# RWKV-7 and dilated attention layer on one core: the RWKV heads' small products alternate between halves of TensorE's array, updates are read out once per two chunks, and low-rank low parts have the full height

## The chip, the cores and the metric

One core of a Trainium2 chip. The core has TensorE (PE, matrix products; PEld is its loading of weights), VectorE (DVE), ScalarE (ACT), GpSimd (POOL), and SyncE (SP), which issues most DMAs. The metric is the time of one execution on the device in microseconds (us), the median of several runs.

## The reference

A decoder layer for 2048 tokens of 1024 channels: eight RWKV-7 heads and eight heads of dilated attention side by side, an output projection, and a SwiGLU feed-forward. The change touches the RWKV heads alone; their core is a recurrence over tokens:

```python
def step(state, inp):
    r_t, w_t, k_t, v_t, kk_t, a_t = inp
    sa = jnp.einsum('bhij,bhj->bhi', state, -kk_t)
    state = (state * w_t[:, :, None, :]
             + sa[..., :, None] * (kk_t * a_t)[..., None, :]
             + v_t[..., :, None] * k_t[..., None, :])
    y = jnp.einsum('bhij,bhj->bhi', state, r_t)
    return state, y
...
w = -jax.nn.softplus(-(w0 + jnp.tanh(xw) @ w2)) - 0.5
decay = jnp.exp(-jnp.exp(w.astype(jnp.float32)))
a = jax.nn.sigmoid(a0 + xa @ a2)
```

`w2` and `a2` are low-rank products: 64 channels in, 512 out.

## The kernel before

The tokens are taken in 4 blocks of 512. TensorE's order is written out by hand: `drive` lays two streams into one. The dense stream (`dense_in`: input projection, in float32r products of 128 x 128 by 512 columns; three products, `three`, for each pair of high and low parts) fills the time in which the messy stream (`rwkv`) waits for other engines. A step of the messy stream yields the dense time to put before the next one (Y_T, CH_X and so on, in us); these numbers set the order, whatever the products really take. The other engines' instructions are ordered by a scheduler. When the dense stream ends, during the last block's chunks, attention becomes the other stream.

The heads go through TensorE as 4 pairs; a pair holds one head in channels 0 to 63 and one in 64 to 127 (e = 0, 1). For each block and pair:

- `start_pair` makes decay and learning rate (lines 519 to 526): a product at full height with the high part of `w2`, one on half the height (64 rows) with its low part `wa_lo`, and the same for `a2`.
- The T blocks (L638): products over 64 rows, 128 columns wide, for each of 8 chunks of 64 tokens, in 4 batches (e = 0, 1; chunks 0 to 3, 4 to 7) of 4 products. Each batch writes one tile `tp` of the pool `ps_t`, which has two buffers and serves other small products too. Two ScalarE copies (L645, L646) and two VectorE products with triangle masks (L648, L652) empty it.
- After an inversion on VectorE, merges (L705, L718) of 32 x 32 blocks: 4 batches a block, each 16 products on rows 0 to 31 and then 16 on rows 64 to 95.

Then the chain over the 8 chunks. A chunk has five groups of products, 8 each (4 pairs, e = 0, 1): `xp` (L804, all rows, column half e), the readout of the state `ye[e]` (L819, row half e, column half by the chunk's parity q), `up_` (L829, row half e, column half e), the new state `s_ps` (L842, all rows, column half e), and the readout of the updates, into the same `ye[e]` (L861, all rows, column half q). VectorE turns `s_ps` into the state for the next chunk (L848, L857, tile `suv`), for which the next `xp` waits. A product of float32 operands is two instructions on TensorE.

Of the kernel before, what the change touches and what calls it, by code (L numbers as in the profile page):

```python
# [9 lines left out]
F32 = mybir.dt.float32  # L10
# [8 lines left out]
P = 128  # L19
# [22 lines left out]
def f32(ap):  # L42
    return ap.bitcast(F32)
# [3 lines left out]
def tile_hybrid_layer(  # L47
# [29 lines left out]
    # TensorE takes its instructions as they come here: the two streams are laid out below.  # L77
# [22 lines left out]
    # Additive masks over [previous block | own block], and over the own block in the order of  # L100
    # the second branch with the keys of the third: same residue mod 4, not later.
    amask = cst.tile([P, 2 * P], BF16, name="amask")
    mask4 = cst.tile([P, P // 4, 4], BF16, name="mask4")

    def build_masks():
        res = cst.tile([P, 4], F32, name="res")
        nc.vector.tensor_reduce(out=res, in_=ident.rearrange("p (a c) -> p c a", c=4), axis=AX.X, op=ALU.max)
        nc.vector.tensor_scalar(out=res, in0=res, scalar1=-1.0, scalar2=-NEG, op0=ALU.add, op1=ALU.mult)
        nc.vector.tensor_copy(out=mask4, in_=res.unsqueeze(1).to_broadcast([P, P // 4, 4]))
        nc.gpsimd.memset(amask, 0.0)  # L110
        m4 = mask4.rearrange("p a c -> p (a c)")
        for m, sign in ((amask[:, 0:P], 1), (amask[:, P:], -1), (m4, -1)):
            nc.gpsimd.affine_select(
                out=m, in_=m, pattern=[[sign, P]], base=0, channel_multiplier=-sign,
                compare_op=ALU.is_ge, fill=NEG,
            )

    # Per-channel vectors, one row per 128 channels, turned to columns.
# [20 lines left out]
    def rms_inv(pool, ss, scale, eps, who):  # L139
        """(ss * scale + eps) ** -0.5 on [128, n]."""  # L140
# [38 lines left out]
    class Weights:  # L179
        """Pieces of weights in the order of their use: loaded and split ahead of it."""  # L180
# [57 lines left out]
    # Constants of this part.  # L238
# [7 lines left out]
    ones64 = chp.tile([P, CH], F32, name="ones64")  # L246
    maskS = chp.tile([P, CH], F32, name="maskS")
    maskI = chp.tile([P, CH], F32, name="maskI")
    headsel = sp.tile([P, 2], F32, name="headsel")
    reset = sp.tile([P, TB], BF16, name="reset")  # L250
# [3 lines left out]
    wa_lo = sp.tile([P, W], F32R, name="wa_lo")  # L254
# [10 lines left out]
    def constants():  # L265
# [5 lines left out]
        # high parts twice, low parts of one beside those of the other  # L271
        for hi, src, tag, lo in ((w2d, decay_w2[0], "L", slice(0, HD)), (a2d, iclr_a2[0], "kkh", slice(HD, P))):
# [4 lines left out]
            nc.vector.tensor_tensor(out=wa_lo[lo], in0=raw[lo], in1=f32(hi[lo]), op=ALU.subtract)  # L277
# [7 lines left out]
        nc.gpsimd.memset(reset, 1.0)  # L285
        nc.gpsimd.memset(reset.rearrange("p (c t) -> p c t", t=CH)[:, :, 0:1], 0.0)
# [3 lines left out]
        nc.gpsimd.memset(ones64, 1.0)  # L290
        for m, base in ((maskS, -1), (maskI, 0)):
            for h in range(2):
                # keep t - s + base >= 0
# [63 lines left out]
    def dense_in():  # L357
# [58 lines left out]
        for b in range(nblocks):  # L416
            t0 = b * TB
            for at, ct in enumerate(ORDER):
# [26 lines left out]
                if b == 0 and at == 6:  # L445
                    build_masks()
# [1226 lines left out]
```

## Time and profile before

| what | value |
|---|---|
| median of 3 timed runs | 3056.62 us |
| the runs | 3053.95 to 3061.08 us |
| profiled execution, its span | 3063.5 us |
| TensorE busy | 2966.2 us, 97% of the span |
| VectorE, ScalarE, GpSimd busy | 1959.1, 1407.3, 383.5 us |
| granted TensorE clock, mean | 0.981 |

The span is the profiled execution's own time from its first to its last instruction; no time around it is known, and it is 6.9 us longer than the median of the runs without profile. Busy time of TensorE is an upper bound: products are pipelined, and their ends are modelled.

### The profile page before, as it was taken

The numbers are of one execution on the slowest core, as the hardware profiler recorded it, in microseconds if no ns is written. First come the engines' busy times: TensorE is split into PE (matmuls) and PEld (weight loads), VectorE is DVE, ScalarE is ACT, GpSimd is POOL, SyncE is SP. The second block draws the span as 40 slices with busy tenths as digits, with TensorE's granted clock in tenths as the row PEclk, the third lists the DMA queues.
The fourth block names the chain that finished last, engine by engine and source line by source line (L and its number), as shares of the span: only waits on it lengthen the run. The fifth ranks groups of instructions, "written<-read, shape, count | busy, mean of one in ns | idle before, by whom it ended". The sixth has DMA issues, their size and how long they took to land.

```text
span 3063.5 us, 47429 instructions
## 1 busy us (share of the span) xinstructions
PE 2966.2 (97%) x17457; PEld 2449.3 (80%) x17457; DVE 1959.1 (64%) x3974; ACT 1407.3 (46%) x2688; POOL 383.5 (13%) x540
## 2 busy tenths in 40 slices
PE   8999999999998888899999999999999999999998
PEld 6777787787787776788888888888888888888887
DVE  6778777776776886675765676566575544454444
ACT  5434534444444665675554455444454323342223
POOL 1113113203102321100110111001011100000001
PEclk9999999999998898899999999999999999999999
DMA  4332332231232578554544345443434333343333
GB/s 124 90 98 76 90 97 73 85 105 58 68 94 81 158 226 251 174 139 117 145 125 144 114 126 162 122 127 97 135 118 145 98 108 98 100 121 97 97 97 103
DMA packets 456716, 358.67 MB, mean 117 GB/s; under 512 B 26610, under 2 KB 384548, under 8 KB 456484
## 3 DMA queue, kind: packets, MB, share of 16 engines
q1 hardware_dynamic: 419348, 318.35, 35.2%
q10 hardware_dynamic: 32656, 22.62, 2.4%
q0 software_dynamic: 4480, 14.68, 1.3%
q8 instruction: 137, 2.24, 0.3%
q14 instruction: 95, 0.78, 0.1%
HBM read 311.19 MB, written 44.37 MB: 116 GB/s over the span
## 4 chain that ended last, share of the span: by engine, by line
PE 56%; DMA 3%; DVE 2%; ACT 1%; issue 1%; POOL 0%; SPq 0%; ACTq 0%; DVEq 0%; POOLq 0%
PE acc L214 6%; PE acc L216 6%; PE acc L215 6%; PE pg L214 5%; PE pu L214 5%; PE pg L216 5%; PE pu L216 5%; PE pu L215 5%; PE pg L215 5%; PE po L963 3%; PE pt_att L949 2%; PE s_att L932 1%; PE s_att L933 1%; DMA rq<-qT 1%; DMA rk_all<-kT 1%
## 5 line engine op out<-in xcount | busy, mean ns | idle before, releaser
L202 DVE TENSOR_TENSOR wlo<-wraw,whi 128x512 fp32r<-128x512 f32 x800 | 564.6, 707 | 631.1 <-ACT whi L200 623.5
L200 ACT CAST whi<-wraw 128x512 fp32r<-128x512 f32 x800 | 495.0, 619 | 961.1 <-PE acc L216 251.1
L214 PE MATMUL pd<-h_hi,whi 128*128 128x512 f32 (+1 forms) x840 | 357.0, 425 | 2.9 <-DVE r L456 1.5
L216 PE MATMUL pd<-h_hi,wlo 128*128 128x512 f32 (+1 forms) x840 | 332.0, 395 | 0.0
L215 PE MATMUL pd<-h_lo,whi 128*128 128x512 f32 (+1 forms) x840 | 331.0, 394 | 0.9 <-DVE h_lo L374 0.6
L214 PE MATMUL acc<-whi,a_hi 128*128 128x512 f32 x704 | 286.6, 407 | 0.6 <-DVE x L1487 0.5
L214 PE MATMUL pg<-fh_hi,whi 128*128 128x512 f32 x704 | 284.1, 404 | 1.0 <-DVE x L1487 0.6
L214 PE MATMUL pu<-fh_hi,whi 128*128 128x512 f32 x704 | 284.6, 404 | 0.0
L216 PE MATMUL pg<-fh_hi,wlo 128*128 128x512 f32 x704 | 275.9, 392 | 0.2 <-DVE wlo L202 0.2
L216 PE MATMUL acc<-whi,a_lo 128*128 128x512 f32 x704 | 276.0, 392 | 0.0
L216 PE MATMUL pu<-fh_hi,wlo 128*128 128x512 f32 x704 | 275.8, 392 | 0.0
L215 PE MATMUL pg<-fh_lo,whi 128*128 128x512 f32 x704 | 274.6, 390 | 0.0
L215 PE MATMUL acc<-wlo,a_hi 128*128 128x512 f32 x704 | 274.5, 390 | 0.0
L215 PE MATMUL pu<-fh_lo,whi 128*128 128x512 f32 x704 | 274.4, 390 | 0.0
L942 ACT ACTIVATE pr<-pr,mx 128x256 f32<-128x256 f32 (+1 forms) x416 | 162.5, 449 | 102.6 <-DVE mx L937 102.4
L214 PEld LDWEIGHTS pd<-h_hi,whi 128*128 128x128 f32 x840 | 160.3, 191 | 43.7 <-issue 3.6
L216 PEld LDWEIGHTS pd<-h_hi,wlo 128*128 128x128 f32 x840 | 160.0, 191 | 35.4
L215 PEld LDWEIGHTS pd<-h_lo,whi 128*128 128x128 f32 x840 | 160.7, 191 | 27.1 <-DVE h_lo L374 2.2
L969 POOL COPY oo<-mx 128x2 f32<-128x2 f32 (+2 forms) x160 | 51.6, 328 | 996.2 <-DVE mx L937 888.6
L963 PEld LDWEIGHTS po<-vv,pts 128*128 128x128 f32 x1008 | 152.6, 196 | 21.7 <-ACT oo L968 2.6
L216 PEld LDWEIGHTS pg<-fh_hi,wlo 128*128 128x128 f32 x704 | 132.1, 188 | 30.0 <-DVE wlo L202 1.0
L216 PEld LDWEIGHTS pu<-fh_hi,wlo 128*128 128x128 f32 x704 | 132.1, 188 | 29.4 <-DVE wlo L202 0.3
(578 smaller groups left out, 5684.0 us busy)
## 6 DMA issues: line engine op xcount, KB each, us to landing
wraw<-in_w_in_dram SPq DMA_DIRECT2D x208, 256.0 KB, 2.9
wraw<-in_w_gate_dram SPq DMA_DIRECT2D x176, 256.0 KB, 2.9
wraw<-in_w_up_dram SPq DMA_DIRECT2D x176, 256.0 KB, 2.9
wraw<-in_w_down_dram SPq DMA_DIRECT2D x176, 256.0 KB, 2.6
rq<-qT SPq DMA_DIRECT2D x128, 128.0 KB, 3.6
wraw<-in_w_out_dram SPq DMA_DIRECT2D x64, 256.0 KB, 3.1
rk_all<-kT SPq DMA_DIRECT2D x48, 256.0 KB, 4.2
rk_all<-kT SPq DMA_DIRECT2D x80, 128.0 KB, 3.4
```

Source lines behind the costliest of these rows:

```text
L200: nc.scalar.copy(out=hi, in_=raw)
L202: nc.vector.tensor_tensor(out=lo, in0=raw, in1=f32(hi), op=ALU.subtract)
L214: nc.tensor.matmul(ps, lhsT=lhs[0], rhs=rhs[0], start=first, stop=False)
L215: nc.tensor.matmul(ps, lhsT=lhs[0], rhs=rhs[1], start=False, stop=False)
L216: nc.tensor.matmul(ps, lhsT=lhs[1], rhs=rhs[0], start=False, stop=last)
L932: nc.tensor.matmul(ps[:, g, :], lhsT=q, rhs=kh, start=True, stop=False)
L933: nc.tensor.matmul(ps[:, g, :], lhsT=q, rhs=kl, start=False, stop=True)
L942: nc.scalar.activation(out=pr[:, g, :], in_=pr[:, g, :], func=AF.Exp, scale=-1.0, bias=mx[:, g])
L949: nc.tensor.transpose(pt[:, g, kb, :], pr[:, g, kb * P : (kb + 1) * P], ident)
L963: nc.tensor.matmul(po[:, g, :], lhsT=pts[:, g, kb, :], rhs=vb[g][kb], start=(kb == 0), stop=(kb == kbs - 1))
L969: nc.gpsimd.tensor_copy(out=o[:, :, OA:OW], in_=self.mxs[j])
```

## The change

The core of the difference; lines that only lose comments, or get new numbers, are left out.

```diff
-                nc.tensor.matmul(zp, lhsT=wa_lo[0:HD, js], rhs=xwa[0:HD, 0], start=False, stop=True)
+                nc.tensor.matmul(zp, lhsT=w2lo[:, js], rhs=xwa[:, 0], start=False, stop=True)
...
-                nc.tensor.matmul(ap_, lhsT=wa_lo[HD:P, js], rhs=xwa[HD:P, 1], start=False, stop=True)
+                nc.tensor.matmul(ap_, lhsT=a2lo[:, js], rhs=xwa[:, 1], start=False, stop=True)
...
-                for e in range(2):
-                    es = slice(e * HD, (e + 1) * HD)
-                    ks = slice((1 - e) * HD, (2 - e) * HD)
-                    for c0 in range(0, NCH, 4):
-                        tp = ps_t.tile([P, 4, 2, CH], F32, name="tp", tag="t")
-                        for c in range(4):
+                for c0 in range(0, NCH, 4):
+                    tps = [ps_t.tile([P, 4, 2, CH], F32, name="tp", tag="t") for _ in range(2)]
+                    for c in range(4):
+                        for e, tp in enumerate(tps):
+                            es = slice(e * HD, (e + 1) * HD)
                             nc.tensor.matmul(
                                 tp[:, c, :, :], lhsT=BK[es, c0 + c, :, :],
                                 rhs=Wj[es, c0 + c, 2 * e : 5 : 4 - 2 * e, :], start=True, stop=True,
                             )
...
-                        yield Y_T
+                    yield Y_T2
...
-                for e in range(2):
-                    r0 = e * HD
-                    for u in range(U2):
+                for u in range(U2):
+                    for r0 in (0, HD):
                         nc.tensor.matmul(
                             qp[r0 + 32 : r0 + 64, u, :], lhsT=TAB[r0 : r0 + 32, g + u, 32:64],
...
-                    for j in range(NPAIR):
+                for j in range(NPAIR):
+                    for e in range(2):
+                        es = slice(e * HD, (e + 1) * HD)
                         nc.tensor.matmul(
                             ye[e][qs, j, :], lhsT=Wt[j][es, c, 4, :], rhs=now[es, j, e, :],
...
-                for e in range(2):
-                    for j in range(NPAIR):
-                        nc.tensor.matmul(
-                            ye[e][qs, j, :], lhsT=Wt[j][:, c, 2 * e + 1, :], rhs=now[:, j, e, :],
-                            start=False, stop=True, skip_group_check=True,
-                        )
+                if q == 1:
+
+                    for e in range(2):
+                        for j in range(NPAIR):
+                            for cc, of in ((c - 1, before), (c, now)):
+                                nc.tensor.matmul(
+                                    ye[e][(cc % 2) * CH : (cc % 2 + 1) * CH, j, :],
+                                    lhsT=Wt[j][:, cc, 2 * e + 1, :], rhs=of[:, j, e, :],
+                                    start=False, stop=True, skip_group_check=True,
+                                )
+                before = now
```

Y_T2 is 1.6, twice Y_T. The low parts `w2lo` and `a2lo` have 128 rows, of which GpSimd sets the other 64 to zero at the start. The second merge (`mp`) alternates like the first. The triangle masks become bf16 and the reset of the decay's running sum becomes bytes. Attention's masks, built in the first block before, are built in attention's own pool where attention begins.

TensorE's order at the first pair's T blocks (L638, in the change L647; `tp` is their tile, `pd` the dense stream's). Before:

```order
L638 MATMUL tp<-W_547,BK 128x128 x4
L214 MATMUL pd<-h_hi,whi 128x512
L215 MATMUL pd<-h_lo,whi 128x512
L216 MATMUL pd<-h_hi,wlo 128x512
...
L638 MATMUL tp<-W_547,BK 128x128 x4
...
L666 MATMUL tp_788<-ident,BK 128x128 x4
```

In the change:

```order
L647 MATMUL tp<-W_548,BK 128x128 x8
L221 MATMUL pd<-h_hi,whi 128x512
L222 MATMUL pd<-h_lo,whi 128x512
L223 MATMUL pd<-h_hi,wlo 128x512
...
L647 MATMUL tp<-W_548,BK 128x128 x8
...
L677 MATMUL tp_775<-ident,BK 128x128 x4
```

Before, 6, 3 and 3 dense products stood between the four batches and 3 before the transposes; now 9 stand between the two batches and 6 before the transposes.

VectorE's order in the same place (L648 and L652, in the change L659 and L663, empty `tp`; L202, now L209, splits weights; `kx` and `mshift` belong to the dense stream). Before:

```order
L648 TENSOR_TENSOR W_547<-tp,maskS 64x4x64
L652 TENSOR_TENSOR W_547<-tp,maskI 128x4x64
L580 SCALAR_TENSOR_TENSOR tmp<-r,vec,tmp 128x512
L648 TENSOR_TENSOR W_547<-tp,maskS 64x4x64
L652 TENSOR_TENSOR W_547<-tp,maskI 128x4x64
L202 TENSOR_TENSOR wlo<-wraw,whi 128x512
L456 SCALAR_TENSOR_TENSOR kx<-pd,omu,mshift 128x512
```

In the change:

```order
L659 TENSOR_TENSOR W_548<-tp,maskS 64x4x64
L663 TENSOR_TENSOR W_548<-tp,maskI 128x4x64
L659 TENSOR_TENSOR W_548<-tp,maskS 64x4x64
L663 TENSOR_TENSOR W_548<-tp,maskI 128x4x64
L209 TENSOR_TENSOR wlo<-wraw,whi 128x512
L466 SCALAR_TENSOR_TENSOR kx<-pd,omu,mshift 128x512
```

Both tiles of a batch are now emptied one behind the other, and the split and the dense stream's evacuation stand ahead of the next batch's masks.

TensorE's order in an even and the next odd chunk (`y_2043` and `y_2044`, in the change `y_2030` and `y_2031`, are `ye[0]` and `ye[1]`). Before, at the end of either chunk:

```order
L842 MATMUL s_ps<-suv,BKT_1396 64x64 x2
L861 MATMUL y_2043<-suv,W_547 64x64
L861 MATMUL y_2043<-suv,W_778 64x64
L861 MATMUL y_2043<-suv,W_992 64x64
L861 MATMUL y_2043<-suv,W_1213 64x64
L861 MATMUL y_2044<-suv,W_547 64x64
L861 MATMUL y_2044<-suv,W_778 64x64
```

In the change, the end of the even chunk, the next chunk's readout of the state, and the end of the odd chunk:

```order
L853 MATMUL s_ps<-suv,BKT_1383 64x64 x2
L221 MATMUL pd<-h_hi,whi 128x512
...
L830 MATMUL y_2030<-suv,W_548 64x64
L830 MATMUL y_2031<-suv,W_548 64x64
...
L853 MATMUL s_ps<-suv,BKT_1383 64x64 x2
L875 MATMUL y_2030<-suv,W_548 64x64 x2
L875 MATMUL y_2030<-suv,W_765 64x64 x2
...
L875 MATMUL y_2031<-suv,W_548 64x64 x2
```

In the even chunk dense products follow `s_ps` directly; the odd one reads out both chunks' updates.

## Rows read from the trace of the kernel before

**Rows 1.** The profile's page: its span, and engines' busy time (us, share, instructions).

```profile
span 3063.5 us, 47429 instructions
PE 2966.2 (97%) x17457; PEld 2449.3 (80%) x17457; DVE 1959.1 (64%) x3974; ACT 1407.3 (46%) x2688; POOL 383.5 (13%) x540
```

**Rows 2.** Windows: stretch, its length; busy of PE, PEld, DVE, ACT, POOL; clock, DMA.

```profile
60.00:145.00 85.00, 85.00 (x446) 66.36 (x445) 62.41 (x122) 43.94 (x93) 12.11 (x16) 1.00 0.28 84
945.00:1030.00 85.00, 71.67 (x826) 62.32 (x824) 61.01 (x160) 47.92 (x115) 27.32 (x38) 0.86 0.33 96
```

**Rows 3.** Timeline of TensorE at a T block: start, length (us), instructions merged.

```profile
64.32 0.39 PE L215 MATMUL pd<-h_lo,whi 128*128 128x512 f32 x1
64.55 0.40 PE L216 MATMUL pd<-h_hi,wlo 128*128 128x512 f32 x1
64.88 1.16 PE L638 MATMUL tp<-W,BK 64*128 64x128 f32 x8
65.96 0.50 PE L214 MATMUL pd<-h_hi,whi 128*128 128x512 f32 x1
...
67.54 1.16 PE L638 MATMUL tp<-W,BK 64*128 64x128 f32 x8
```

**Rows 4.** Timeline of the engines that empty this tile, in brackets idle time before.

```profile
65.21 0.69 DVE L202 TENSOR_TENSOR wlo<-wraw,whi 128x512 fp32r<-128x512 f32 x1
...
66.07 0.36 ACT L645 COPY TAB<-tp 32x256 f32<-32x256 f32 x1 [1.34 <-PE tp L638]
...
66.44 0.26 ACT L646 COPY TAB<-tp 32x128 f32<-32x128 f32 x1
...
66.73 0.43 DVE L648 TENSOR_TENSOR W<-tp,maskS 64x256 f32<-64x256 f32 x1 [0.83 <-ACT TAB L646]
...
67.17 0.42 DVE L652 TENSOR_TENSOR W<-tp,maskI 128x256 f32<-128x256 f32 x1
```

**Rows 5.** Timeline of TensorE, low-rank products of a pair: first, and dense product after.

```profile
41.67 0.39 PE L520 MATMUL zp<-xwa,w2d 128*128 128x512 f32 x1
...
43.28 0.51 PE L214 MATMUL pd<-h_hi,whi 128*128 128x512 f32 x1
```

**Rows 6.** Timeline of TensorE over the first chunk of the first block.

```profile
199.01 0.96 PE L819 MATMUL y<-suv,W 64*64 64x64 f32 x16
199.91 0.50 PE L214 MATMUL pd<-h_hi,whi 128*128 128x512 f32 x1
...
201.50 0.68 PE L829 MATMUL up__2073<-xs,TAB 64*64 64x64 f32 x16
202.11 0.50 PE L214 MATMUL pd<-h_hi,whi 128*128 128x512 f32 x1
...
204.38 0.69 PE L842 MATMUL s_ps<-suv,BKT 128*64 128x64 f32 x16
204.89 1.10 PE L861 MATMUL y<-suv,W 128*64 128x64 f32 x16
205.92 0.50 PE L214 MATMUL pd<-h_hi,whi 128*128 128x512 f32 x1
```

**Rows 7.** Windows within one batch of L819: length, busy (instructions in flight), clock, DMA.

```profile
208.12:208.42 0.30, 0.30 (x6) 1.00 0.00 0
208.42:208.72 0.30, 0.30 (x12) 1.00 0.00 0
```

**Rows 8.** Timeline: L857 and L804 at the first, L804 at the last of 12 chunks.

```profile
205.57 0.87 DVE L857 TENSOR_TENSOR suv<-st,s0p 64x256 f32<-64x256 f32 x2
...
207.50 0.69 PE L804 MATMUL xp<-suv,W 128*64 128x64 f32 x16
...
760.64 1.04 PE L804 MATMUL xp<-suv,W 128*64 128x64 f32 x16 [1.07 <-DVE suv L857]
```

**Rows 9.** Timeline of TensorE at the first merge batch.

```profile
181.40 2.11 PE L705 MATMUL qp<-M,TAB 32*32 32x32 f32 x64
183.44 0.50 PE L214 MATMUL pd<-h_hi,whi 128*128 128x512 f32 x1
```

More of the change, by code (lines that the diff above doesn't have):

```diff
@@ L98, in tile_hybrid_layer, with build_mask @@
     nc.gpsimd.memset(neg_half, -0.5)
[L102 to L109, printed above, removed]
+    def build_mask(pool):
+        amask = pool.tile([P, 2 * P], BF16, name="amask")
         nc.gpsimd.memset(amask, 0.0)
-        m4 = mask4.rearrange("p a c -> p (a c)")
-        for m, sign in ((amask[:, 0:P], 1), (amask[:, P:], -1), (m4, -1)):
+        for m, sign in ((amask[:, 0:P], 1), (amask[:, P:], -1)):
             nc.gpsimd.affine_select(
@@ L116, in build_masks, with build_mask4 @@
             )
+        return amask
+    def build_mask4(pool):
+        mask4 = pool.tile([P, P // 4, 4], BF16, name="mask4")
+        res = pool.tile([P, 4], F32, name="res")
+        nc.vector.tensor_reduce(out=res, in_=ident.rearrange("p (a c) -> p c a", c=4), axis=AX.X, op=ALU.max)
+        nc.vector.tensor_scalar(out=res, in0=res, scalar1=-1.0, scalar2=-NEG, op0=ALU.add, op1=ALU.mult)
+        nc.vector.tensor_copy(out=mask4, in_=res.unsqueeze(1).to_broadcast([P, P // 4, 4]))
+        m4 = mask4.rearrange("p a c -> p (a c)")
+        nc.gpsimd.affine_select(
+            out=m4, in_=m4, pattern=[[-1, P]], base=0, channel_multiplier=1, compare_op=ALU.is_ge, fill=NEG,
+        )
+        return m4
     rows = (
@@ L244, in load_gain @@
             nc.sync.dma_start(out=t, in_=mix_norm_g[0:1, h * W : (h + 1) * W].to_broadcast([P, W]))
-    ones64 = chp.tile([P, CH], F32, name="ones64")
-    maskS = chp.tile([P, CH], F32, name="maskS")
-    maskI = chp.tile([P, CH], F32, name="maskI")
+    maskS = chp.tile([P, CH], BF16, name="maskS")
+    maskI = chp.tile([P, CH], BF16, name="maskI")
     headsel = sp.tile([P, 2], F32, name="headsel")
-    reset = sp.tile([P, TB], BF16, name="reset")
+    reset = sp.tile([P, TB], mybir.dt.uint8, name="reset")
     g2 = [chp.tile([P, W], F32R, name=f"g2{part}") for part in ("hi", "lo")]
@@ L253, in tile_hybrid_layer @@
     a2d = sp.tile([P, W], F32R, name="a2d")
-    wa_lo = sp.tile([P, W], F32R, name="wa_lo")
+    w2lo = sp.tile([P, W], F32R, name="w2lo")
+    a2lo = sp.tile([P, W], F32R, name="a2lo")
     lnw = chp.tile([P, W], F32, name="lnw")
@@ L270, in constants @@
             at += n
-        for hi, src, tag, lo in ((w2d, decay_w2[0], "L", slice(0, HD)), (a2d, iclr_a2[0], "kkh", slice(HD, P))):
+        for hi, low, src, tag, lo, zero in (
+            (w2d, w2lo, decay_w2[0], "L", slice(0, HD), slice(HD, P)),
+            (a2d, a2lo, iclr_a2[0], "kkh", slice(HD, P), slice(0, HD)),
+        ):
+            nc.gpsimd.memset(f32(low[zero]), 0.0)
             raw = sp.tile([P, W], F32, name="wa_raw", tag=tag)
@@ L276, in constants @@
             nc.scalar.copy(out=hi, in_=raw)
-            nc.vector.tensor_tensor(out=wa_lo[lo], in0=raw[lo], in1=f32(hi[lo]), op=ALU.subtract)
+            nc.vector.tensor_tensor(out=low[lo], in0=raw[lo], in1=f32(hi[lo]), op=ALU.subtract)
         raw = sp.tile([P, W], F32, name="g2_raw", tag="qkv", bufs=1)
@@ L284, in constants @@
         nc.gpsimd.memset(carry, 0.0)
-        nc.gpsimd.memset(reset, 1.0)
-        nc.gpsimd.memset(reset.rearrange("p (c t) -> p c t", t=CH)[:, :, 0:1], 0.0)
+        nc.gpsimd.memset(reset, 1)
+        nc.gpsimd.memset(reset.rearrange("p (c t) -> p c t", t=CH)[:, :, 0:1], 0)
         nc.gpsimd.memset(headsel, 0.0)
@@ L289, in constants @@
         nc.gpsimd.memset(headsel[HD:P, 1:2], 1.0)
-        nc.gpsimd.memset(ones64, 1.0)
+        for m in (maskS, maskI):
+            nc.gpsimd.memset(m, 1.0)
         for m, base in ((maskS, -1), (maskI, 0)):
@@ L641, in rwkv @@
                             )
-                        us = slice(j * NCH + c0, j * NCH + c0 + 4)
+                    us = slice(j * NCH + c0, j * NCH + c0 + 4)
+                    cs = slice(c0, c0 + 4)
+                    for e, tp in enumerate(tps):
+                        ks = slice((1 - e) * HD, (2 - e) * HD)
                         h0, h1 = slice(e * HD, e * HD + 32), slice(e * HD + 32, e * HD + 64)
@@ L714, in rwkv @@
                 mp = ps_c.tile([P, U2, 32], F32, name="mp", tag="c")
-                for e in range(2):
-                    r0 = e * HD
-                    for u in range(U2):
+                for u in range(U2):
+                    for r0 in (0, HD):
                         nc.tensor.matmul(
```

13 lines of the change are left out of this document (6 added, 7 removed).

## The prediction, made before the result was known

> **What bounds the kernel now.** The page comes first: TensorE is busy for 97% of a span of 3063.5 us [rows 1]. That share says little about a single stage, so the windows by stage come next. In 60 to 145 us, where the products of the RWKV heads stand between those of the input projection, TensorE is never idle, VectorE is busy for 62.41 of 85 us and ScalarE for 43.94: no other engine is near its limit, and time taken from TensorE there comes off the span. In 945 to 1030 us, where the last head chunks run beside the first attention units, TensorE is busy for 71.67 of 85 us: it waits there, and shorter products bring little [rows 2]. So I price the edits in TensorE's own timeline, by the start of a batch and the start of what follows, since the ends are modelled and overlap.
>
> **Reading the small products.** The timeline of one T block gives the unit: dense products start 0.23 us apart, a change to products on half of the array's height costs 0.10 more (64.55 to 64.88), and a batch of 8 instructions (4 products, two instructions each) takes 1.08 us until the dense stream is back [rows 3]. In the chain stand batches of 16 small instructions. Those that alternate between halves are short: L829, whose rows and columns alternate, takes 0.61 us, and L842, whose columns alternate, 0.51. Those that stay on one half are long: L861 takes 1.03, L819 takes 0.90 [rows 6]. Without the 0.10 for the change of shape, 0.032 us an instruction against 0.058. No batch alternates rows alone, as the T blocks and L819 will, but L819 shows it once: it goes from the upper to the lower row half in its middle, and there 12 instructions are in flight in 0.3 us, against 6 at its start [rows 7]. The lower half starts while the upper still works, in the same columns. I take it that alternating row halves run at once.
>
> **T blocks.** Before, each of 16 pairs of heads (4 blocks, 4 pairs) has 4 batches: 4 x (0.10 + 1.08) = 4.72 us. After, 2 batches of 16, with 8 instructions on each half; if the halves run at once each takes what 8 took and one short step: 2 x (0.10 + 1.09) = 2.38. That frees 2.34 x 16 = 37.4 us. If they take turns, a batch of 16 costs about 2 x 1.08 - 0.20 and only the changes of shape are saved, 0.30 a batch, 9.6 us.
>
> The Trainium skill, page "TensorE: Matmul & The Clock Gate", section "Measured speedup vs the span model", gives 3.07 times for four row tiles, not four; scaled to two, 1.53 in place of 2, a batch would take some 1.37 us, an estimate. No run here shows it; the rule stands among the rivals.
>
> **What the T blocks give back.** A batch now fills both buffers of the pool at once. A tile is emptied by two ScalarE copies and then two VectorE products: the batch ends at 66.04 and the last reader at 67.59, 1.55 us later, 0.85 of it VectorE's [rows 4]. With two tiles ready together, the second waits for VectorE: 1.17 + 1.55 + 0.85 = 3.57 us after the batch began. TensorE comes to the next batch after 1.09 and nine dense products; six took 67.54 - 65.96 = 1.58 [rows 3], so nine 2.27: 3.36. That is a wait of 0.2 to 0.3. The transposes after the second batch come at 1.09 + 1.58 - 0.10 = 2.57 and want the first tile, free at 2.72: 0.15 to 0.2. Together 0.45 x 16 = 7 us. Twice, V's transposes stand close behind a batch and want the same pool: 1.6 and 0.7 us. I take 10 us back, between 5 (the waits fall within the signals' own time) and the rival's price below.
>
> **Low parts.** The four products of a pair start at 41.67 and the dense stream is back at 43.28: 1.61 us for what at 0.23 each takes 0.92, because each alternates with one on half the height [rows 5]. Padded with zeros all have the full height: 0.69 x 16 = 11.0 us. The zeros are two memsets at the start, behind which nothing on GpSimd hurries, and the readers of the results stand behind dense products as before. This term has no condition.
>
> **Readout of the state (L819).** Alternating, 0.90 becomes what L829 takes, 0.61: 0.29 a chunk. Of 32 chunks I count 25, without the seven of the last block that lie in the waiting stretch: 7.2 us.
>
> **Readout of updates (L861).** In an even chunk the batch goes: L842 and L861 took 0.51 + 1.03 = 1.54, L842 alone with its change of shape 0.61 [rows 6]; 0.93 is freed. In an odd one L861 has 32 instructions over both column halves: 0.51 + 32 x 0.032 + 0.10 = 1.63, 0.09 more. For 12 pairs of chunks (three blocks) that is 10.1 us. But the 1.03 us in an even chunk covered something. The state goes on by VectorE: L857 ended at 206.44, and the next L804 began at 207.50, with 1.06 to spare [rows 8]. So the first of 12 odd chunks loses nothing; at the last, TensorE already waits 1.07 us for L857 [rows 8], and what is freed there turns into a longer wait. Summed over these 12 starts, cover of 0.93 against what is spare at each, 6.6 us go back. I take 3.5, between 0 and 10.
>
> **Merges.** A batch of 64 takes 2.04 us, 0.030 an instruction [rows 9]. Rows and columns alternate after: by the ratio of the chain 0.016, 16 x 63 x 0.015 = 15 us less. But the shortest mean distance in any row is 0.032, L842's, and no row shows TensorE starting small products closer over a batch. Between 0 and 15 I take the middle, 8.
>
> The Trainium skill, same page, section "Wait — 56ns, not 53.3ns?", puts a floor of about 25 ns under the distance of starts: by it the merges give some 5 us, an estimate, and the sum falls by 3. The trace neither reaches nor refutes it.
>
> **The masks.** Attention's masks are built where attention begins. GpSimd and VectorE have idle time there, and TensorE waits anyhow for the first keys. The triangle masks in bf16 and the reset in bytes leave the number of elements as it is. I take nothing for these, at most 1 us either way, covered by the waiting stretch of [rows 2].
>
> **Sum.** 37.4 - 10 + 11.0 + 7.2 + 3.5 + 8 = 57.1 us. The profiled execution, 3063.5, would become 3006; it lies 6.9 above the median of the timed runs, 3056.62, so for these 3000. 0.2% of it, 6 us, is about what a measurement of this kernel can tell from no change.
>
> **Rivals.**
> *Halves overlap incompletely.* If row halves give 1.53 and not 2, each of 32 T batches takes 0.28 more: 9 us, 3009. For it speaks only that no batch of row halves has been run whole.
> *Emptying the T tiles is slower than their arithmetic.* VectorE also splits weights, 0.69 us each [rows 4]. If one stands ahead of the masks at both waits of a pair, 32 x 0.69 = 22 us more: 3022. In the new order no split stands between the masks of one batch, but one does ahead of the next batch's.
> *Row halves take turns.* The T blocks then save 9.6 - 10, the state's readout nothing, the merges perhaps 4, low parts and updates as above: 18 us, 3038. Against it speak [rows 7].
> *It does nothing,* as all freed time returns as waits for VectorE or ScalarE: 3057. Their shares in [rows 2] speak against it.
> *Slower: the T tiles hold TensorE up.* Both buffers stand full until VectorE is through; from 1.8 us of extra wait at each of 32 batches on, the whole gain of 57 is gone. Three instructions of the kind of the split ahead of the masks, 2.07, give 32 x 2.07 = 66 us, 3066. VectorE's 62 of 85 leaves room, so this needs an unlucky order at every batch.
>
> **Chances and range.** Forecast 0.60, incomplete overlap 0.10, slower emptying 0.12, turns 0.10, nothing 0.03, slower 0.05. The likeliest alone runs from 2984 (merges 15, updates 10) to 3014 (neither). The range takes in the next two cases with the merges at their best, 2982 to 3030, and leaves out the last three, 0.18. Faster: 0.92.
>
> **What would show it.** T batches of 16 at 1.1 us, not 2; waits of 0.2 to 0.3 us before every second one, put down to VectorE's masks; the four low-part products within 0.92; L819's successor at 0.61; a longer idle time before L804 in odd chunks; merge batches between 1.0 and 2.04. From 1030 us of before on, the distance of the two traces should stay as it is. The prediction is wrong if row halves don't run together, or if the T tiles are emptied later than the order lets me expect.

## The result, and the profile after

The changed kernel takes 3003.81 us (median of 4 runs, 2999.32 to 3009.42) against 3057.05 for the kernel before beside it (4 runs, 3053.95 to 3061.08): a ratio of 0.9829, 95% interval 0.9814 to 0.9844, or 53 us. It was forecast at 3000. The profiled executions differ by 62.2 us. Part of the 9 us between the two figures can be TensorE's clock, told here by its mean granted share of 2.4 GHz: the profiled execution of the kernel before had 0.981, the median of its 17 timed runs beside e9 to e11 is 0.985, and all four runs of the changed kernel have 0.982. A step of 0.001 in this mean, 6 us of 3000 at 1.2 instead of 2.4 GHz, is worth 3 us at most.

The page of the changed kernel, the lines that answer to [rows 1]:

```profile
span 3001.3 us, 47441 instructions
PE 2881.1 (96%) x17457; PEld 2381.6 (79%) x17457; DVE 1957.3 (65%) x3974; ACT 1405.2 (47%) x2688; POOL 383.7 (13%) x543
```

TensorE's busy time fell by 85.1 us and the span by 62.2: of what the products freed, 23 us came back as idle time. The window of the T blocks (columns as in [rows 2]) shows the same in little:

```profile
60.00:145.00 85.00, 83.78 (x486) 67.22 (x485) 70.24 (x145) 46.97 (x99) 13.59 (x18) 1.00 0.33 96
```

Here TensorE was never idle before; now it is for 1.2 us, and VectorE is busy for 70 of 85 us instead of 62, because the same work stands closer.

Timelines of TensorE in the changed kernel: two T batches, the low parts, parts of the second chunk, a merge batch. They answer to [rows 3], [rows 5], [rows 6] and [rows 9]; columns are start, length (us), instructions merged, and in brackets idle time before.

```profile
63.78 1.16 PE L647 MATMUL tp<-W,BK 64*128 64x128 f32 x16
64.88 0.50 PE L221 MATMUL pd<-h_hi,whi 128*128 128x512 f32 x1
...
67.21 0.46 PE L647 MATMUL tp<-W,BK 64*128 64x128 f32 x2
67.86 1.13 PE L647 MATMUL tp<-W,BK 64*128 64x128 f32 x14 [0.20 <-DVE W L663]
68.92 0.50 PE L221 MATMUL pd<-h_hi,whi 128*128 128x512 f32 x1
```

```profile
42.18 0.39 PE L530 MATMUL zp<-xwa,w2d 128*128 128x512 f32 x1
...
43.11 0.39 PE L221 MATMUL pd<-h_hi,whi 128*128 128x512 f32 x1
```

```profile
172.00 1.20 PE L715 MATMUL qp<-M,TAB 32*32 32x32 f32 x64
173.13 0.50 PE L221 MATMUL pd<-h_hi,whi 128*128 128x512 f32 x1
...
194.63 0.68 PE L830 MATMUL y<-suv,W 64*64 64x64 f32 x16
195.24 0.50 PE L221 MATMUL pd<-h_hi,whi 128*128 128x512 f32 x1
...
199.94 1.10 PE L875 MATMUL y<-suv,W 128*64 128x64 f32 x32
200.98 0.50 PE L221 MATMUL pd<-h_hi,whi 128*128 128x512 f32 x1
```

Start to start: a batch of 16 instructions on both row halves takes 1.10 us, 8 on one half took 1.08. The low parts take 0.93, the state's readout 0.61, the update products of two chunks (32 instructions) 1.04, a merge batch 1.13 instead of 2.04. All products got as short as forecast, within 0.01 us, or shorter. The second T batch shows the price: after two instructions, which are its first product, on one row half, it stops until VectorE is through with the tile of the other half (67.21 to 67.86), and it takes 1.71 us, not 1.10.

Where TensorE waits now: groups by line for 0 to 1110 us (busy us, mean ns of one | idle us before them and what ended it).

```profile
L647 PE MATMUL tp<-W,BK 64*128 64x128 f32 x512 | 42.3, 285 | 5.0 <-DVE W L663 4.1 <-ACT whi L207 0.4 <-DVE carry L469 0.2
L813 PE MATMUL xp<-suv,W 128*64 128x64 f32 x512 | 27.3, 238 | 14.7 <-DVE suv L868 13.7 <-ACT suv L749 0.3
...
L499 PE MATMUL pv<-ident,qkv 128*128 128x128 f32 x64 | 9.6, 273 | 2.4 <-DVE W L663 2.4
```

In the kernel before, `xp` was L804:

```profile
L804 PE MATMUL xp<-suv,W 128*64 128x64 f32 x512 | 24.0, 228 | 4.8 <-DVE suv L857 4.4
```

The waits at the T tiles (L647 and L499) were expected. The 13.7 us before the chain's first product `xp` were not, in this form: 4.4 stood there before, the forecast let 6.6 be added, but 12.2 of the 13.7 lie in four waits of 2.8 to 3.4 us (at 213.7, 254.9, 693.4 and 716.8), where the kernel before waited 0.2 to 1.1. What is late is the pair of state sums L868; the timeline of VectorE ahead of one such wait says why.

```profile
210.06 0.69 DVE L785 TENSOR_TENSOR y<-y,gn_r 128x512 f32<-128x512 f32 x1 [1.77 <-POOL gn_r L152]
210.79 0.69 DVE L789 TENSOR_TENSOR y<-y,lnw 128x512 f32<-128x512 f32 x1
211.51 0.69 DVE L791 TENSOR_TENSOR bv<-y,bv 128x512 f32<-128x512 f32 x1
212.12 0.68 DVE L209 TENSOR_TENSOR wlo<-wraw,whi 128x512 fp32r<-128x512 f32 x1
212.72 0.42 DVE L859 TENSOR_TENSOR st<-s_ps,pc 128x256 f32<-128x256 f32 x1
213.17 0.87 DVE L868 TENSOR_TENSOR suv<-st,s0p 64x256 f32<-64x256 f32 x2
```

and TensorE meanwhile:

```profile
208.28 0.69 PE L853 MATMUL s_ps<-suv,BKT 128*64 128x64 f32 x16
...
213.74 1.04 PE L813 MATMUL xp<-suv,W 128*64 128x64 f32 x16 [3.17 <-DVE suv L868]
```

The state product is done before 209, but `st` (L859), its reader, begins at 212.72. VectorE first stands idle for 1.77 us, waiting for GpSimd's power for the group norm of the chunks before; then come the norm's tail (L785, L789, L791) and a split of weights. The tail is not urgent, the state is. In the kernel before, the same place reads:

```profile
224.56 0.69 DVE L780 TENSOR_TENSOR y<-y,lnw 128x512 f32<-128x512 f32 x1
225.17 0.42 DVE L848 TENSOR_TENSOR st<-s_ps,pc 128x256 f32<-128x256 f32 x1
225.50 0.68 DVE L782 TENSOR_TENSOR bv<-y,bv 128x512 f32<-128x512 f32 x1
226.10 0.86 DVE L857 TENSOR_TENSOR suv<-st,s0p 64x256 f32<-64x256 f32 x2
```

There, L776 and L780 (now L785 and L789) stood ahead of `st` too, but the addition of `bv` (now L791) came behind `st` and the split behind the sums, and TensorE had the updates of the even chunk to do meanwhile.

### The profile page after: what moved, and what is told of

It is laid out like the page before. It is cut to its first block, busy times and chain, and to the rows that moved or that the text cites. A ratio compares the mean times of both kernels' runs of the same rounds, so it can differ in the third digit from the quotient of the medians.

```text
span 3001.3 us, 47441 instructions
## 1 busy us (share of the span) xinstructions
PE 2881.1 (96%) x17457; PEld 2381.6 (79%) x17457; DVE 1957.3 (65%) x3974; ACT 1405.2 (47%) x2688; POOL 383.7 (13%) x543
## 5 line engine op out<-in xcount | busy, mean ns | idle before, releaser
L209 DVE TENSOR_TENSOR wlo<-wraw,whi 128x512 fp32r<-128x512 f32 x800 | 566.0, 708 | 618.4 <-ACT whi L207 613.3
L221 PE MATMUL pd<-h_hi,whi 128*128 128x512 f32 (+1 forms) x840 | 350.6, 417 | 3.4 <-DVE r L466 1.6
L222 PEld LDWEIGHTS pd<-h_lo,whi 128*128 128x128 f32 x840 | 159.8, 190 | 28.6 <-DVE h_lo L386 2.6
```

What stands on the lines that cost most here:

```text
L209: nc.vector.tensor_tensor(out=lo, in0=raw, in1=f32(hi), op=ALU.subtract)
L221: nc.tensor.matmul(ps, lhsT=lhs[0], rhs=rhs[0], start=first, stop=False)
L222: nc.tensor.matmul(ps, lhsT=lhs[0], rhs=rhs[1], start=False, stop=False)
```

## The experiments

Each kernel was timed beside the kernel before, whose medians there were 3057.13 to 3059.01. The gain or loss below is the difference of a run's median from 3003.81, from that of e3 where it starts from e3, and from the kernel before beside it (3058.38) for e9 and e10. The intervals of the ratios are about 0.0015 wide to either side, 4 to 5 us, so a difference of two medians is sure to some 6 us.

| run | starts from | edit | median us | ratio to before, 95% | difference |
|---|---|---|---|---|---|
| e1 | changed | merges as before | 3021.34 | 0.9877 (0.9862 to 0.9892) | +17.5 |
| e2 | changed | updates read out every chunk | 2998.82 | 0.9807 (0.9792 to 0.9821) | -5.0 |
| e3 | changed | norm's tail behind the state sums | 2986.78 | 0.9765 (0.9750 to 0.9779) | -17.0 |
| e4 | changed | T blocks as before | 3030.16 | 0.9909 (0.9893 to 0.9924) | +26.4 |
| e5 | changed | low parts as before | 3018.00 | 0.9870 (0.9850 to 0.9889) | +14.2 |
| e6 | changed | state readout as before | 3013.46 | 0.9854 (0.9837 to 0.9871) | +9.7 |
| e7 | e3 | updates read out every chunk | 2995.75 | 0.9800 (0.9783 to 0.9816) | +9.0 |
| e8 | e3 | 1.0 us of cover moved between the T batches | 2980.38 | 0.9747 (0.9731 to 0.9763) | -6.4 |
| e9 | before | norm's tail behind the state sums | 3056.94 | 1.0002 (0.9991 to 1.0013) | -1.4 |
| e10 | before | merges alternate | 3037.87 | 0.9938 (0.9925 to 0.9950) | -20.5 |
| e11 | e3 | 1.6 us of cover moved between the T batches | 2982.32 | 0.9751 (0.9738 to 0.9764) | -4.5 |
| e12 | e3 | 1.2 us between, 0.8 us behind the T batches | 2976.21 | 0.9730 (0.9714 to 0.9746) | -10.6 |

### Undoing one part at a time: e4, e5, e6

The T blocks' loops as before the change, `e` outside, four batches of 8 instructions a pair:

```diff
-                for c0 in range(0, NCH, 4):
-                    tps = [ps_t.tile([P, 4, 2, CH], F32, name="tp", tag="t") for _ in range(2)]
-                    for c in range(4):
-                        for e, tp in enumerate(tps):
...
+                for e in range(2):
...
+                    for c0 in range(0, NCH, 4):
+                        tp = ps_t.tile([P, 4, 2, CH], F32, name="tp", tag="t")
+                        for c in range(4):
...
```

> The changed kernel, but the T blocks run as before: one half of the rows after the other, four batches of 8 products a pair of heads with dense products between each. Theory (the two halves run at the same time, and the second tile's emptying costs 6.5 us of waits): 31 us slower, about 3035 us, a batch of 8 takes 1.08 us plus 0.20 us for two changes of form, and the waits ahead of the T batches, the turns of V and those of B and K fall by 6 us. Rival A (the waits are smaller and half of them belongs to the turns anyway): 37 us slower, 3041 us. Rival B (half of the gain was something else, the clock or the order on VectorE): 20 us slower or less.

26.4 us slower, 28.6 in the profiled spans. The group by line of this kernel that answers to L647 above:

```profile
L649 PE MATMUL tp<-W,BK 64*128 64x128 f32 x512 | 73.9, 285 | 0.0
```

The waits go (those at L499 too), the busy time comes back. The theory's 31 us was too much: it took the waits from the idle rows alone (4.1 + 2.4). Added up over the 16 second batches of the changed kernel, from a batch's start to the next instruction's, they take 25.1 us, 7.7 more than 16 times 1.09, since most of the wait inside a batch lies under products still in flight. With 2.5 us idle ahead of these batches and 2.4 at L499 the waits are 12.6 us, and 37.4 - 12.6 = 24.8. Rival B falls.

The low parts on 64 rows again:

```diff
-                nc.tensor.matmul(zp, lhsT=w2lo[:, js], rhs=xwa[:, 0], start=False, stop=True)
+                nc.tensor.matmul(zp, lhsT=w2lo[0:HD, js], rhs=xwa[0:HD, 0], start=False, stop=True)
...
-                nc.tensor.matmul(ap_, lhsT=a2lo[:, js], rhs=xwa[:, 1], start=False, stop=True)
+                nc.tensor.matmul(ap_, lhsT=a2lo[HD:P, js], rhs=xwa[HD:P, 1], start=False, stop=True)
```

> The changed kernel, but the low parts of the two low-rank products run on 64 rows, as before. Theory (a change of form inside a pair of products costs what the rows of before show): 11 us slower, 3015 us; a pair takes 1.61 us instead of 0.92. Rival A (the T stage gave 39.3 us in the comparison of the traces, 25.3 of them are the T blocks by the run that undid these, so the low parts gave 13 to 14): 13.5 us slower, 3017 us. Rival B (the form change lay beside waiting work): 5 us or less.

14.2 us slower, 13.8 in the spans, against 11.0 from the theory and 13.5 from rival A; the two are closer together than the measurement is sure. The trace tells more. A mark behind the work of all 16 pairs is the last merge batch ahead of the fourth block's chain: it starts at 882.22 in the changed kernel and at 892.32 in e5, 10.1 us later, and both stood at 1.2 GHz for 20.5 us until then. So the products are worth about what the theory said; the other 4 us come behind the mark, where e5 has some 10 us more at 1.2 GHz than the changed kernel, worth 5 at most. That padded products are no slower is plain from the 0.93 us above. The state's readout with `e` outside `j`:

```diff
-                for j in range(NPAIR):
-                    for e in range(2):
-                        es = slice(e * HD, (e + 1) * HD)
+                for e in range(2):
+                    es = slice(e * HD, (e + 1) * HD)
+                    for j in range(NPAIR):
```

> The changed kernel, but the state readout runs one half of the rows after the other, as before. Theory (the two halves run at the same time, a batch takes 0.90 us instead of 0.61, and little waits on it): 7 to 9 us slower, 3011 to 3013 us. Rival A (what the batch loses is cover for ScalarE's copy of the first product, so a wait ahead of the next product takes it back): 3 us slower or less.

9.7 us slower (12.0 in the spans), a little over the theory; rival A, that the gain comes back as a wait, is out.

### The merges and the clock: e1, e10

In e1 the merges of the changed kernel take one row half after the other again; in e10 the kernel before gets only the new order of the merges. The edit is the same, there and back, in both merge loops:

```diff
-                for u in range(U2):
-                    for r0 in (0, HD):
+                for r0 in (0, HD):
+                    for u in range(U2):
```

> The changed kernel, but each merge batch of 64 runs its products one half of the rows after the other, as before. Theory (merges give 14.5 us by their own products, and the half clock that stood behind the second merge of the later blocks gave back another 8.6 us): some 23 us slower than the changed kernel, so about 3027 us; a merge batch takes 2.04 us, the second merge product batch of blocks 1 to 3 about 2.9 us, and the granted clock there falls to half. Rival A (the products alone count, the half clock was an accident of the run or is moved elsewhere): 14.5 us slower, 3018 us, no stretch at half clock behind the merges. Rival B (the forecast's size): 8 us slower, 3012 us.

> The kernel before, with only the merges' products alternating between the halves. Theory (14.5 us of products, and the half clock behind the second merge of blocks 1 to 3 goes with the sequence that came ahead of it): 19 to 24 us faster, 3033 to 3038 us, and the granted clock stays at full speed behind the merges. Rival A (the products alone): 14 to 15 us faster, 3042 us. Rival B (the forecast's size): 8 us faster, 3049 us.

17.5 us slower, and 20.5 faster. The products give 16 x (2.04 - 1.13) = 14.5 of that. For the rest the trace shows a place. Windows of 6.8 us, the first two of the kernel before, in the middle of the second merge's last batch in blocks 1 and 2 and on from there (the eighth column is the granted clock):

```profile
436.72:443.52 6.80, 6.80 (x56) 5.76 (x53) 2.62 (x5) 1.83 (x4) 0.00 (x0) 0.50 0.05 16
685.76:692.56 6.80, 6.80 (x38) 5.57 (x36) 3.20 (x5) 0.36 (x1) 0.00 (x0) 0.51 0.13 39
```

and those at the same places in e10:

```profile
430.84:437.64 6.80, 6.80 (x62) 5.54 (x57) 4.80 (x12) 4.03 (x10) 2.24 (x3) 1.00 0.38 118
674.95:681.75 6.80, 6.80 (x61) 5.53 (x57) 5.97 (x12) 2.31 (x5) 0.77 (x1) 1.00 0.23 62
```

In the kernel before TensorE was granted 1.2 GHz there, and dense products stood 0.43 us apart instead of 0.23, although TensorE was busy throughout: it had come from four batches of 64 instructions (32 products of 32 x 32), 2.04 us each, with three to six dense products between. In the first block the same four batches left the clock at 2.4 GHz, so they don't bring it down every time. With batches of 1.13 us it stays at 2.4 GHz in all four blocks. In e1 the half clock is back behind the second merge of two blocks, 3.4 us in the third and 6.8 in the fourth; in the kernel before it was 6.8 us in each of three. So the merges were worth 14.5 us by their products, and 3 to 6 more by this clock, as far as the two runs tell. The mean granted clocks go with that: 0.980 in e1's runs against 0.982, 0.987 in e10's against 0.985. The forecast's size (8) was too little. e1 stays under its theory's 23 us, and the clock's share is smaller than what a comparison is sure to, so its size is not shown.

### What VectorE's order costs: e3, e9, e2, e7

e3 is the changed kernel with one edge: the tail of the norm is queued on VectorE behind the last state sums.

```diff
-                    nc.vector.tensor_tensor(out=nxt[es, :, e, :], in0=st[es], in1=s0p[es], op=ALU.add)
+                    lead[:] = [nc.vector.tensor_tensor(out=nxt[es, :, e, :], in0=st[es], in1=s0p[es], op=ALU.add)]
...
-                pin(nc.vector.tensor_tensor(
-                    out=y, in0=y, in1=rstd.unsqueeze(2).to_broadcast([P, HEADS, HD]), op=ALU.mult
-                ))
+                with tc.issue_after(lead[0].ins):
+                    nc.vector.tensor_tensor(
+                        out=y, in0=y, in1=rstd.unsqueeze(2).to_broadcast([P, HEADS, HD]), op=ALU.mult
+                    )
```

> The changed kernel, with one edge more: on VectorE the tail of the group norm (times rstd, times lnw, plus bv) is queued behind the two state sums of the chunk before it. Theory (the long waits ahead of a chunk's first product come from VectorE's order): the four waits of about 3 us and the half clock behind them vanish, idle time of TensorE ahead of the first product falls from 13.7 us to at most 4 us, and the time falls by 6 to 14 us, to 2990 to 2998 us. Rival A (the waits only move: the tail ends later, the gate's bank comes free later, and the transposes of V or the state product wait for it): within 3 us of the changed kernel. Rival B (the order is not the cause, the cover is too short): the waits stay and the time too.

17.0 us faster, more than the theory gave. VectorE at the same place as above, in e3:

```profile
208.49 0.69 DVE L209 TENSOR_TENSOR wlo<-wraw,whi 128x512 fp32r<-128x512 f32 x1 [0.52 <-ACT whi L207]
209.10 0.42 DVE L860 TENSOR_TENSOR st<-s_ps,pc 128x256 f32<-128x256 f32 x1
209.56 0.87 DVE L869 TENSOR_TENSOR suv<-st,s0p 64x256 f32<-64x256 f32 x2
```

The wait of 3.17 us is gone: the sums end at 210.43, where they ended at 214.04, and the tail follows them. In the group of `xp` the idle time falls from 14.7 to 6.9 us, not to the 4 of the theory:

```profile
L814 PE MATMUL xp<-suv,W 128*64 128x64 f32 x512 | 26.1, 235 | 6.9 <-DVE suv L869 5.7 <-ACT suv L749 0.3
```

The other 9 of 17 us can nearly all be clock again. By the mark e3 is 15.7 us ahead (866.48 against 882.22), and until there the changed kernel stood at 1.2 GHz for 20.5 us, e3 for 3.4, a difference worth 8.5 us at most. In the changed kernel each of the four long waits was followed by half clock; windows of it:

```profile
214.70:218.10 3.40, 3.40 (x24) 2.79 (x23) 0.66 (x1) 0.37 (x1) 1.18 (x3) 0.50 0.15 45
692.60:699.40 6.80, 5.97 (x40) 4.96 (x41) 3.47 (x6) 0.37 (x1) 2.69 (x3) 0.50 0.15 41
```

and one of e3, at the first of these places in the program (its one stretch at 1.2 GHz up to the mark, at 685.0, follows a wait of 1.9 us at the third):

```profile
211.10:214.50 3.40, 3.40 (x43) 2.67 (x41) 2.97 (x6) 0.99 (x2) 1.83 (x3) 1.00 0.32 94
```

e9 puts the same edge, alone, into the kernel before.

> The kernel before, with the same edge on VectorE as in the run with the tail behind the state sums, and nothing else. Theory (the edge mends what the change did to VectorE's order, and before that order did little harm: 4.4 us of waits for the state sums): at most 6 us faster than the kernel before, so 3051 to 3057 us, and the gain of 17 us on the changed kernel is for the greater part the change's own harm. Rival (the edge helps every kernel alike): 14 us faster or more, 3043 us or less, and the change did no harm by the order.

Nothing in the time: 3056.94 against 3058.38. But its waits of `xp` for the sums fell from 4.4 to 0.5 us, and its clock is lower: 0.981 in the median of its 12 runs (0.980 to 0.983) against 0.985 in the 17 of the kernel before (0.982 to 0.987), which is worth up to 12 us. The two profiled executions, both at 0.981, differ by 8.6 us (3054.9 and 3063.5). So the edge may well help the kernel before too and lose it to the clock; why the clock is lower, no run shows. As timed, the edge is worth 17 us to the changed kernel and nothing to the kernel before, and in this sense the 17 us are harm of the change. Which part did it, e2 tells; it reads the updates out after every chunk again, and this alone returns VectorE's order in these chunks to that of the kernel before:

```diff
-                if q == 1:
-                    for e in range(2):
-                        for j in range(NPAIR):
-                            for cc, of in ((c - 1, before), (c, now)):
...
+                for e in range(2):
+                    for j in range(NPAIR):
...
```

> The changed kernel, but the updates are read out after every chunk, as before. Theory (reading out once per two chunks gained nothing, because it took cover out of the even chunks and moved VectorE's order): within 4 us of the changed kernel, 3000 to 3008 us; VectorE's order in the chain is that of the kernel before, the four waits of about 3 us ahead of the first product of a chunk shrink to at most 2 us, and the 16 more form changes cost the rest. Rival A (the forecast's term holds): 3.5 us slower, with the waits unchanged. Rival B (the readout is worth all it frees): 10 us slower, 3014 us.

5.0 us faster, a little more than the theory's 4, with 5.5 us of waits for the sums instead of 13.7, and with no stretch at 1.2 GHz up to the mark, where the changed kernel has 20.5 us. Both rivals, which had the readout once per two chunks worth something, fall here. But e7 makes the same edit on e3, where the order can't be harmed:

> The kernel with the tail of the group norm queued behind the state sums (2986.8 us), and with the updates read out after every chunk, as before. Theory (without the harm of VectorE's order the readout once per two chunks is worth something, because it saves 16 changes of form and half of the sequence): 2 to 6 us slower than 2986.8 us. Rival A (the cover lost in the even chunks eats it all): within 1.5 us. Rival B (it harms by more than the order): faster by 2 us or more.

9.0 us slower, more than the theory's 6, and the runs of the two don't overlap (2993.9 to 2999.7 against 2983.9 to 2987.05). So, as timed, the readout once per two chunks gains 9 us with the edge and loses 5 without it: 14 us hang on the order on VectorE, by the waits and by the clock behind them. Where the 9 us lie, the mark tells, in e3 and then in e7:

```profile
866.48 1.20 PE L727 MATMUL mp<-TAB,M 32*32 32x32 f32 x64
```

```profile
868.82 1.20 PE L727 MATMUL mp<-TAB,M 32*32 32x32 f32 x64
```

Only 2.3 us of the 9 arise in the first three blocks, with the same 3.4 us at 1.2 GHz in both. More than half of the 10.1 us that the shorter sequence frees there goes back as lost cover: until the mark, idle time before `xp` is 0.5 us in e7 and 6.2 in e3. By the first attention product behind the last chunk the distance is 2.9 us (954.39 and 957.27), although e7 stands at 1.2 GHz for 5.9 us less between the mark and there, worth 3 at most. And 5.5 us come right behind it, where no head product is left and both run the same products of attention and what follows it, e3 and then e7:

```profile
954.39:1002.12 47.73, 40.82 (x248) 36.09 (x247) 40.41 (x117) 32.44 (x77) 12.20 (x19) 0.85 0.66 210
957.27:1010.48 53.21, 44.69 (x247) 39.05 (x247) 41.26 (x117) 32.65 (x77) 12.20 (x19) 0.81 0.62 197
```

The clock is lower in e7 there, and TensorE idles for 8.5 us instead of 6.9. So some 3 to 6 us are the readout's own in the chain; the cause of the rest stays open.

### The T tiles' waits: e8, e11, e12

The kernel of e3, with dense products moved from ahead of a pair's T blocks (Y_C, Y_L) to between its two T batches; e8 as below, e11 with 3.2, 0.6 and 4.4 in place of 2.6, 1.2 and 5.0.

```diff
-                    yield Y_T2
+                    yield 2.6 if c0 == 0 else Y_T2
...
-    Y_XWA, Y_KX, Y_SQ, Y_F, Y_G, Y_A, Y_C, Y_L, Y_T, Y_T2 = 1.5, 2.0, 1.9, 3.0, 2.4, 1.5, 2.2, 6.0, 0.8, 1.6
+    Y_XWA, Y_KX, Y_SQ, Y_F, Y_G, Y_A, Y_C, Y_L, Y_T, Y_T2 = 1.5, 2.0, 1.9, 3.0, 2.4, 1.5, 1.2, 5.0, 0.8, 1.6
```

> The kernel with the tail of the group norm queued behind the state sums (2986.8 us), and with 1.0 us of dense products moved from ahead of a pair's T blocks to between its two T batches. Theory (the second batch waits for VectorE and ScalarE to empty the second tile, and only for that): the waits in and ahead of the second batch, some 10 us in 16 pairs, fall below 3 us, and the time falls by 6 to 10 us, to 2977 to 2981 us. Rival A (the first batch then comes before its operands are there, or the turns of B and K wait for the tiles in their place): within 2 us of 2986.8 us. Rival B: slower by more than 2 us, since VectorE is the bound in this stage.

> As the run that moved 1.0 us of dense products between the two T batches (2980.4 us), with 1.6 us moved instead. Theory (what was left of the second batch's wait, 5 us over 16 pairs, is still cover that is too short): 2 to 5 us faster, 2975 to 2978 us, and a second batch takes 1.1 us nearly everywhere. Rival (the waits left belong to single late masks and the turns, and the first batch now comes too early): within 2 us of 2980.4 us.

e8 gives 6.4 us (2.8 in the spans), the low end of the theory, and 10 of 16 second batches still take over 1.15 us. In e11 only one does, and yet the time is that of e8: the rival holds. The groups by line of e11 say where the wait went, to the turns of B and K (L677), which want the same two tiles and waited 0.1 us before:

```profile
L647 PE MATMUL tp<-W,BK 64*128 64x128 f32 x512 | 37.6, 285 | 0.5 <-DVE W L663 0.5
...
L677 PE MATMUL tp<-ident,BK 128*128 128x128 f32 x128 | 19.6, 275 | 3.6 <-DVE W L663 1.8 <-ACT ksq L543 0.5
```

So e12 gives both places cover: 2.8 between the batches and 2.4 behind them, Y_C 0.2 and Y_L 4.0.

> As the run that moved 1.6 us of dense products between a pair's two T batches (2982.3 us), but 1.2 us go between them and 0.8 us behind the second, ahead of the turns of B and K, all taken from ahead of the T blocks. Theory (the wait that left the second T batch went to the turns, because they want the same two tiles, and 3.6 us of it stand there): idle time ahead of the turns falls under 1.5 us with that of the T batches staying under 1.5 us, and the time falls by 2 to 5 us, to 2977 to 2980 us. Rival (VectorE's and ScalarE's work on the tiles sets the pace of the stage, so the wait appears ahead of the first batch or elsewhere): within 2 us of 2982.3 us.

```profile
L647 PE MATMUL tp<-W,BK 64*128 64x128 f32 x512 | 37.7, 285 | 0.4 <-DVE W L663 0.4
...
L677 PE MATMUL tp<-ident,BK 128*128 128x128 f32 x128 | 19.2, 273 | 1.2 <-DVE W L663 1.2
```

Both waits are small, 2.5 us less than in e11 together, and 2976.21 us is the best time measured, 6.1 us under e11, 27.6 under the changed kernel and 2.7% under the kernel before. A third buffer for these tiles, which would take the wait away without moving anything, was not tried.

## Why the prediction was right, and where its steps were not

The time came out 4 us from the forecast. The steps, by undoing each part (medians; in brackets the profiled spans):

| term | forecast | measured |
|---|---|---|
| T blocks, with their waits | 37.4 - 10 = 27.4 | 26.4 (28.6) |
| low parts | 11.0 | 14.2 (13.8) |
| readout of the state | 7.2 | 9.7 (12.0) |
| readout of updates | 3.5 | -5.0 (-3.5) |
| merges | 8 | 17.5 (18.9) |
| sum | 57.1 | 62.7 (69.8), whole change 53.2 (62.2) |

**Row halves at once.** Right, and it carried the forecast. The 12 instructions in flight in [rows 7] were the evidence; a batch of 16 takes 1.10 us against 1.09 worked out. The turns rival wanted twice that. The rule of the Trainium skill cited there ("TensorE: Matmul & The Clock Gate", "Measured speedup vs the span model") would have made it 1.37 us by the estimate that scales four row tiles to two; the trace doesn't agree, the gain of two row halves is two.

**Waits of the T tiles.** Near in size, 10 us against 12.6: 7.7 inside the second batches, 2.5 ahead of them, and 2.4 at V's transposes, where 1.6 and 0.7 were forecast and 1.7 and 0.7 came. The place was half right: the waits are at the second batch and put down to VectorE's masks, but mostly inside it, where it turns to the second tile, 0.6 us or more in ten of 16 pairs rather than 0.2 to 0.3; the transposes of B and K waited 0.1 us in all. The rival of slower emptying, 22 us more, did not come about; e8 to e12 show that it was a matter of cover, since the order of TensorE's stream alone removed it.

**Readout of updates.** The step that failed, though the sum hid it. The forecast priced the lost cover with VectorE's instructions where they stood before. It did not ask whether the scheduler would leave them there. It didn't: the rest of the norm's tail and a split of weights went ahead of the state, and in place of 3.5 us gained the term came out as 5.0 lost, with four waits of about 3 us and half clock behind each. With the order mended it is a gain of 9.0 us (e7). For the first three blocks, which the forecast priced, that is 2.3 where it said 3.5, and 5.7 more of idle time where it said 6.6 us of lost cover; so its arithmetic there was near. The rest lies behind, 0.5 in the last block's chunks and the greater part in attention after them, for a cause that is not shown.

**Merges.** Mis-sized, at the bound that the text itself gave: 14.5 us of products where 8 was taken between 0 and 15, plus the clock, which the forecast did not see in the trace of before though it stands there (window 436.72 above). The shortest distance in its rows was not L842's 0.032 us but the merges' own 0.030, by its own reckoning. A batch of 64 in 1.13 us is under 18 ns an instruction, the change of form included. The Trainium skill, same page, section "Wait — 56ns, not 53.3ns?", has a floor of about 25 ns; the measurement goes below it, and decides.

**Low parts and state.** Right in mechanism, 0.93 and 0.61 us as worked out; the medians are some 3 us above the terms, less than the comparison is sure to. For the low parts the trace gives 10.1 us up to the mark, against 11.0, and the rest stands with the clock behind it. For the state, e6 is 7.0 us behind the changed kernel at the mark (889.21 against 882.22), what the term said, but it has 6.8 us more at 1.2 GHz until there, worth up to 3.4; so the match is partly luck. Then 2.2 us more come in the last block (the first attention product behind the last chunk starts at 977.72 against 968.50), from which the forecast counted one chunk of eight. The window of 945 to 1030 us in [rows 2] was read too simply: an engine idle for a sixth of a stretch can still gain from shorter work there.

**The masks** were not tried by themselves. The bounds of the rivals (nothing, slower) played no part: neither VectorE nor ScalarE became the limit of a stage. Behind the heads the distance of the two traces was to stay as it is: it is 57.0 us at the first attention product behind the last chunk (1025.50 and 968.50), 61.8 at 1077.51 of before, and 62.2 at the end, so it moved by some 5 us more.

So an error of about +9 us in the merges and the small ones in low parts and state stood against one of 8.5 in the updates, and the sum was right for more than one wrong reason: that it came within 4 us is luck to this extent. (The bounds of the likeliest case, 2984 and 3014, were added up loosely; its own terms give 2986 and 3011.) The parts add up to 62.7 us where the whole gave 53.2. The undone kernels differ in something that belongs to no part, how long TensorE ran at 1.2 GHz: in the profiled executions the mean granted clock is 0.979 in e1, 0.981 in e4, e5 and e6, 0.982 in the changed kernel, 0.986 in e2. Together that could make up some 6 of the 9.5 us (9 + 3 x 3 for the slower clocks, less 12 for e2); that it does is not shown.

## What to carry to other kernels

Price a batch of small products by the start of the batch and of what follows it, and look for halves of the array that stand idle: two row halves in alternation cost what one costs, and a product padded to full height costs less than a change of form. A product that leaves a chain takes its cover with it, and may let a scheduler reorder another engine that nobody edited: compare the order of the engine that the chain waits for before and after, and queue the work that isn't urgent behind the work that is. Compare the granted clock of two kernels before a small difference of their times is put down to an edit, as in e9. When a wait at a shared pool is removed, look at the pool's next user before the gain is counted, as in e11.

## What the runs showed of the hardware that was not expected

TensorE fell to 1.2 GHz while it was busy without a gap, in the last of four batches of 64 instructions on 32 x 32 blocks, with dense products between (window 436.72, kernel before; in three blocks of four), and not when these batches took 1.13 instead of 2.04 us (window 430.84, e10). It also fell after waits of about 3 us (window 214.70), and removing the wait removed the fall (window 211.10, e3). Instructions on 32 x 32 blocks in float32 whose rows and columns alternate between halves start less than 18 ns apart, in the mean of a batch of 64 (1.13 us).
